# A trunk kernel whose first RMS norm is scaled in transposed form, with dummy products while x loads and a new order of the first transfers

## The chip, the cores and the metric

The kernel runs on one core of one Trainium2 chip. A core has a matrix engine (TensorE, PE in the rows; PEld is its weight load), VectorE (DVE), ScalarE (ACT), GpSimd (POOL) and SyncE (SP), a large on-chip buffer of 128 partitions (SBUF), and eight PSUM banks of 128 x 512 float32 in which products are summed. Engines run their own lists of instructions in order and wait for one another on semaphores. The metric is the device time of one execution in microseconds (us). The kernel before takes 1001.04 us, the median of three runs (1000.92 to 1001.54).

## The reference

A trunk of two layers on 256 tokens of width 1024, all in float32. Each layer is half a SwiGLU feed-forward (FFN), a mixing block (retention, block-sparse attention and a convolution, side by side), and half an FFN again; each of the three starts with an RMS norm of x, and one more norm ends the trunk. The model width is 1024 and an FFN's inner width 2816. This case is about the first norm and the first columns of the first FFN (left out below: the mixing block, whose result is added to x):

```python
def rms_norm(x, g):
    xf = x.astype(jnp.float32)
    y = xf * lax.rsqrt(jnp.mean(xf * xf, -1, keepdims=True) + EPS)
    return (y * g.astype(jnp.float32)).astype(x.dtype)

def swiglu(h, wg, wu, wd):
    return (jax.nn.silu(h @ wg) * (h @ wu)) @ wd

for l in range(DEPTH):
    h = rms_norm(x, ffn1_norm[l])
    x = x + 0.5 * swiglu(h, ffn1_wg[l], ffn1_wu[l], ffn1_wd[l])
    h = rms_norm(x, mix_norm[l])
    ...
    h = rms_norm(x, ffn2_norm[l])
    x = x + 0.5 * swiglu(h, ffn2_wg[l], ffn2_wu[l], ffn2_wd[l])
return rms_norm(x, final_norm)
```

## The kernel before

**Numbers in two parts.** Products keep float32 accuracy by splitting each operand into a high part (a rounded copy, type fp32r) and a low part (what the rounding left). ScalarE writes the high part (`whi` of a weight at L145, `hT` or `hfh` of an activation at L196), VectorE subtracts it from the source to get the low part (`wlo` at L146, `hT` or `hfl` at L197). A product is then three products, high by high, high by low and low by high (`mm3`, L201 to L203), or two of which the first takes both parts of the activation at once (`mm2w`, L207 and L208).

**The stream of weights.** All weights pass in a fixed order through three buffers of 1 MB (`raw`). `fetch` issues a transfer on SyncE's queue; the first two are cut into four parts of 256 KB each. `pump` splits half a buffer (a piece of 1024 columns) into its two parts; at most ten pieces are in store (`WBUFS`). The products call `tick`, which pumps the next piece and moves on the side chains of work that wait for their turn.

**The first norm.** `x` stands in two tiles, `x[0]` and `x[1]`, of 128 tokens each. The norm's vector `g` is loaded in a form in which all 128 partitions hold all 1024 numbers (512 KB). For each half of the columns of `x[t]`, ScalarE squares with a running sum (L338, into `sq`), VectorE multiplies x by g (L339, into `xr`), GpSimd adds the constant and takes the power -1/2 (L344, `r`), VectorE multiplies `xr` by `r` (L348), TensorE transposes four blocks of 128 x 128 into one PSUM bank named `tr` (L354), and `split` (L196, L197) takes the bank of 512 columns out as the high and low parts of `hT`, the transposed activation.

**The first FFN's start.** `first_pair` computes gate and up of the first 256 of 2816 columns: for `x[0]`, then for `x[1]`, eight blocks k of 128 columns of x by three products of 512 columns each (L201 to L203). The chain `gated` then forms `s` and `h` (L401, L402) and transposes `h` (L405). After that `single(j)` runs for j = 2 to 21 with products for both token tiles together (L207, L208), each one bank for the gate (`mm`) and one for up (`tr`); with ScalarE and VectorE joining the two halves of a bank (L212, L213).

**What sets the order.** From L831 on to the end of `first_pair` the program's order is the order in which the code is written, engine by engine (`ordered(True)`), as it is at some later stretches; in the others (`ordered(False)`) a scheduler sets it. In `run`, four pieces are pumped around the norm of `x[0]`, and the transposes of `x[1]` are a side chain (`rest`, started at L852) that counts calls of `tick`: `x[1]`'s first four transposes stand in front of block k6 of `x[0]`, the next four behind k7. Small constants (`pos`, `inv`, `vec`, `decay`, `mask`) are issued in `setup_late`, which is called in the loop's second round, behind `single(5)`, and the next norm's vector is loaded through ScalarE's queue (`nxt.gain()`, L363) into the same buffer `g`.

## Time and profile before

| | |
|---|---|
| median of three runs | 1001.04 us (1000.92 to 1001.54) |
| the profiled execution | 1000.19 us, with a span of 998.4 us |
| mean granted clock of TensorE | 0.998 |
| busy: PE, DVE, ACT, POOL | 981.6 us (98%), 685.5 (69%), 537.9 (54%), 64.1 (6%) |
| moved by DMA | 180.69 MB, a mean of 181 GB/s |

The span is the time from the first to the last instruction of the profiled execution; the execution's own time is 1.8 us more. "Busy" counts the time in which an engine works on an instruction. The busy shares are means over the whole span; the rows below mostly come from its first 80 us. A row of a timeline gives the start, the time, the engine, the line of the code, the operation with output and inputs, and behind "x" how many instructions of the kind stand together; in brackets the idle time before, with what ended it.

### The profile page before, as it was taken

The numbers are of one execution on the slowest core, as the hardware profiler recorded it, in microseconds if no ns is written. First come the engines' busy times: TensorE is split into PE (matmuls) and PEld (weight loads), VectorE is DVE, ScalarE is ACT, GpSimd is POOL, SyncE is SP. The second block draws the span as 40 slices with busy tenths as digits, with TensorE's granted clock in tenths as the row PEclk, the third lists the DMA queues.
The fourth block names the chain that finished last, engine by engine and source line by source line (L and its number), as shares of the span: only waits on it lengthen the run. The fifth ranks groups of instructions, "written<-read, shape, count | busy, mean of one in ns | idle before, by whom it ended". The sixth has DMA issues, their size and how long they took to land.

```text
span 998.4 us, 13763 instructions
## 1 busy us (share of the span) xinstructions
PE 981.6 (98%) x5312; PEld 847.6 (85%) x5312; DVE 685.5 (69%) x1032; ACT 537.9 (54%) x904; POOL 64.1 (6%) x109
## 2 busy tenths in 40 slices
PE   6999999999999999999999999999999999999997
PEld 5888888898998888888888888888989888888885
DVE  6886565569976866666576656566699677666653
ACT  6755555366554755555465545454665456555542
POOL 1000000021141000000000000002100400000000
PEclk9999999999999999999999999999999999999999
DMA  8955554336441855555546555544545347555511
GB/s 309 347 194 201 175 204 156 142 122 214 170 170 64 302 204 172 201 177 199 181 173 218 179 193 186 188 150 139 186 143 197 138 148 253 175 204 174 205 44 43
DMA packets 28722, 180.69 MB, mean 181 GB/s; under 512 B 3440, under 2 KB 3824, under 8 KB 10480
## 3 DMA queue, kind: packets, MB, share of 16 engines
q1 hardware_dynamic: 27360, 176.07, 50.7%
q10 hardware_dynamic: 1296, 3.74, 1.0%
q8 instruction: 42, 0.69, 0.3%
q14 instruction: 24, 0.20, 0.1%
HBM read 178.74 MB, written 1.05 MB: 180 GB/s over the span
## 4 chain that ended last, share of the span: by engine, by line
PE 90%; DVE 6%; DMA 1%; ACT 1%; issue 1%; SPq 0%; POOL 0%; POOLq 0%; ACTq 0%; DVEq 0%
PE tr L207 15%; PE mm L207 15%; PE acc L451 8%; PE acc L448 8%; PE acc L447 8%; PE tr L208 7%; PE mm L208 7%; PE mm L201 4%; PE mm L202 4%; PE mm L203 4%; DVE wlo L146 3%; DVE ac L695 2%; PE acc L207 1%; PE tr L354 1%; PE acc L638 1%
## 5 line engine op out<-in xcount | busy, mean ns | idle before, releaser
L146 DVE TENSOR_TENSOR wlo<-raw,whi 128x1024 fp32r<-128x1024 f32 (+2 forms) x348 | 403.3, 1171 | 184.1 <-ACT whi L145 180.3
L145 ACT ACTIVATE whi<-raw 128x1024 fp32r<-128x1024 f32 (+2 forms) x348 | 348.6, 1013 | 229.0 <-PE acc L451 92.3
L207 PE MATMUL tr<-hT,whi 128*128 128x512 f32 x640 | 228.0, 397 | 0.2 <-DVE hfl L197 0.2
L207 PE MATMUL mm<-hT,whi 128*128 128x512 f32 x640 | 227.3, 396 | 0.0
L208 PE MATMUL mm<-hT,wlo 128*128 128x256 f32 x640 | 178.7, 279 | 0.0
L208 PE MATMUL tr<-hT,wlo 128*128 128x256 f32 x640 | 178.7, 279 | 0.0
L207 PEld LDWEIGHTS tr<-hT,whi 128*128 128x128 f32 x640 | 120.2, 188 | 29.2 <-PE mm L208 0.4
L207 PEld LDWEIGHTS mm<-hT,whi 128*128 128x128 f32 x640 | 120.2, 188 | 28.5
L447 PE MATMUL acc<-whi,hfh 128*128 128x512 f32 x352 | 139.2, 395 | 0.0
L448 PE MATMUL acc<-wlo,hfh 128*128 128x512 f32 x352 | 138.7, 394 | 0.0
L208 PEld LDWEIGHTS mm<-hT,wlo 128*128 128x128 f32 x640 | 120.6, 189 | 1.5
L208 PEld LDWEIGHTS tr<-hT,wlo 128*128 128x128 f32 x640 | 120.7, 189 | 0.0
L451 PE MATMUL acc<-whi,hfl 128*128 128x512 f32 x352 | 115.8, 396 | 0.0
L201 PE MATMUL mm<-whi,hT 128*128 128x384 f32 (+1 forms) x288 | 106.7, 371 | 0.7 <-ACT hT L196 0.7
L203 PE MATMUL mm<-whi,hT 128*128 128x384 f32 (+1 forms) x288 | 101.2, 351 | 0.0
L202 PE MATMUL mm<-wlo,hT 128*128 128x384 f32 (+1 forms) x288 | 101.1, 351 | 0.0
L447 PEld LDWEIGHTS acc<-whi,hfh 128*128 128x128 f32 x352 | 66.5, 189 | 15.1
L451 PEld LDWEIGHTS acc<-whi,hfl 128*128 128x128 f32 x352 | 66.3, 188 | 15.2
L448 PEld LDWEIGHTS acc<-wlo,hfh 128*128 128x128 f32 x352 | 66.3, 188 | 13.7
L433 ACT ACTIVATE s<-part 128x256 f32<-128x256 f32 x80 | 33.2, 414 | 79.2 <-DVE part L213 79.1
L213 DVE TENSOR_TENSOR part<-part,tr 128x256 f32<-128x256 f32 x80 | 33.6, 420 | 47.1 <-ACT part L212 47.1
L201 PEld LDWEIGHTS mm<-whi,hT 128*128 128x128 f32 x288 | 54.7, 190 | 5.5 <-issue 1.3
(151 smaller groups left out, 954.2 us busy)
## 6 DMA issues: line engine op xcount, KB each, us to landing
raw<-in_wgb SPq DMA_DIRECT2D x80, 1024.0 KB, 4.9
raw<-in_wd SPq DMA_DIRECT2D x44, 1024.0 KB, 4.9
raw<-in_win SPq DMA_DIRECT2D x28, 768.0 KB, 4.6
raw<-in_wout SPq DMA_DIRECT2D x8, 1024.0 KB, 4.8
raw<-in_wga SPq DMA_DIRECT2D x6, 1024.0 KB, 5.3
raw<-in_wcv SPq DMA_DIRECT2D x4, 1024.0 KB, 4.8
raw<-in_wga SPq DMA_DIRECT2D x8, 256.0 KB, 6.9
g<-in_fgain ACTq DMA_DIRECT2D x3, 512.0 KB, 3.5
```

What stands on the lines that cost most here:

```text
L145: nc.scalar.activation(hi[:, c], src, AF.Copy)
L146: nc.vector.tensor_tensor(lo[:, c], src, hi[:, c].bitcast(F32), op=OP.subtract)
L201: mm(out, ah, wh, start=start, stop=False)
L202: mm(out, ah, wl, start=False, stop=False)
L203: mm(out, al, wh, start=False, stop=stop)
L207: mm(out, wh, x, start=start, stop=False)
L208: mm(out[:, :S], wl, x[:, 0], start=False, stop=stop)
L213: self.nc.vector.tensor_tensor(v, lo, ps[:, :S], op=OP.add)
L433: nc.scalar.activation(s, v, AF.Silu)
L447: mm(ys[t][h], hi[:, ts], wh[:, n], start=first, stop=False)
L448: mm(ys[t][h], hi[:, ts], wl[:, n], start=False, stop=False)
L451: mm(ys[t][h], lo[:, ts], wh[:, n], start=False, stop=last)
```

## The change

The first norm gets code of its own, `start`, in the place of the lines L832 to L852.

- `gcol` is the first norm's vector as a tile of 128 partitions by 8 columns (4 KB), loaded through ScalarE's queue behind `ident`. The vector is no longer loaded in its 512 KB form.
- `spin(16)` is sixteen products of 512 columns on a tile `z` of ones (bf16, in the buffer of `sq`) into a bank `tr`, which nobody reads.
- `first_stats` squares as before but leaves out the multiplication by g; the second addition for `r` stands on VectorE. VectorE scales the first half of the columns by `r`; the second half is scaled on ScalarE for `x[0]` and on VectorE for `x[1]`.
- `first_T` takes each of the four blocks of a bank out by itself: a ScalarE copy with the column of `gcol` as its scale, then on VectorE (block times column) minus the high part.
- The order is new: the second weight piece is pumped between the two banks of `x[0]`, the norm of `x[1]` begins behind both banks, and the transposes of `x[1]` stand in front of block k4 (first four) and of block k6 of `x[0]`.
- `x[1]` is loaded in two transfers. `setup_late` waits, through a one-column copy on GpSimd into each constant's tile, for an `hf` tile of the first pair, and issues each constant behind it.
- The buffer `g` has no user before the next norm, so that norm's vector (`mgain`) is issued where nothing precedes it on ScalarE's queue.

```diff
@@ fetch
             if (i, j) == (0, 1):
-                self.nc.sync.dma_start(self.x[1], self.a["x"][1])
+                for h in range(2):
+                    c = slice(h * 512, (h + 1) * 512)
+                    self.nc.sync.dma_start(self.x[1][:, c], self.a["x"][1][:, c])
@@ setup, setup_late
         self.ident = self.load("ident", (P, P), eng=nc.scalar)
-
-    def setup_late(self):
-        self.pos = self.load("pos", (P, NT), I32)
-        self.inv = self.load("inv", (P, 40))
-        self.vec = self.load("vec", (P, NVEC))
-        self.decay = self.load("decay", (P, H * 2 * P))
+        self.gcol = self.load("gcol", (P, KT), eng=nc.scalar)
+
+    def spin(self, n):
+        ps = self.trb()
+        z = self.act.tile([P, 512], BF16, tag="sq", bufs=1, name=self.name("z"))
+        self.nc.vector.memset(z, 1.0)
+        for _ in range(n):
+            self.nc.tensor.matmul(ps, z[:, :P], z, start=True, stop=True)
+
+    def first_stats(self, t, n):
+        nc = self.nc
+        n["xr"] = n["tile"]()
...
+        for h in range(2):
+            sq = self.act.tile([P, 512], BF16, tag="sq", bufs=1, name=self.name("sq"))
+            nc.scalar.activation(sq, self.x[t][:, h * 512:(h + 1) * 512], AF.Square, scale=1.0 / 32.0, accum_out=ss[:, h:h + 1])
+        nc.gpsimd.tensor_scalar(e, ss[:, 0:1], EPS, None, op0=OP.add)
+        nc.vector.tensor_tensor(e, ss[:, 1:2], e, op=OP.add)
+        nc.gpsimd.tensor_tensor(r, e, self.mhalf[:, :1], op=OP.pow)
+        c = slice(0, 512)
+        nc.vector.tensor_scalar(n["xr"][:, c], self.x[t][:, c], r, None, op0=OP.mult)
+
+    def first_T(self, t, h, n, hT):
+        ps = self.trb()
+        for j in range(4):
+            k = 4 * h + j
+            self.nc.tensor.transpose(ps[:, j * P:(j + 1) * P], n["xr"][:, k * P:(k + 1) * P], self.ident)
+        for j in range(4):
+            k = 4 * h + j
+            g = self.gcol[:, k:k + 1]
+            src = ps[:, j * P:(j + 1) * P]
+            hi, lo = [x[:, k, t * P:(t + 1) * P] for x in hT[:2]]
+            self.nc.scalar.activation(hi, src, AF.Copy, scale=g)
+            self.nc.vector.scalar_tensor_tensor(lo, src, g, hi.bitcast(F32), op0=OP.mult, op1=OP.subtract)
+
+    def start(self, st):
+        self.spin(16)
+        self.fetch()
+        n0, n1 = st.state(0), st.state(1)
+        c = slice(512, 1024)
+        self.first_stats(0, n0)
+        self.pump()
+        self.nc.scalar.activation(n0["xr"][:, c], self.x[0][:, c], AF.Copy, scale=n0["r"])
+        self.first_T(0, 0, n0, st.hT)
+        self.pump()
+        self.first_T(0, 1, n0, st.hT)
+        self.first_stats(1, n1)
+        self.nc.vector.tensor_scalar(n1["xr"][:, c], self.x[1][:, c], n1["r"], None, op0=OP.mult)
+        self.pump()
+        self.pump()
+        self.done.add(st.mark(0))
+        self.hold = True
+
+        def rest():
+            yield 2
+            self.first_T(1, 0, n1, st.hT)
+            yield 1
+            self.hold = False
+            self.first_T(1, 1, n1, st.hT)
+            self.done.add(st.mark(1))
+
+        self.spawn(rest())
+
+    def setup_late(self, after):
+        def late(tile, src):
+            v = tile[:, 0:1]
+            self.nc.gpsimd.tensor_copy(v if tile.dtype == F32 else v.bitcast(F32), after[:, 0:1].bitcast(F32))
+            self.nc.sync.dma_start(tile, src)
+
         c = self.const
+        for n, shape, dt in (("pos", (P, NT), I32), ("inv", (P, 40), F32), ("vec", (P, NVEC), F32), ("decay", (P, H * 2 * P), F32)):
+            t = c.tile(list(shape), dt, tag=n, name=n)
+            late(t, self.a[n])
+            setattr(self, n, t)
...
-            self.nc.sync.dma_start(mask, self.a["mask"])
+            late(mask, self.a["mask"])
@@ ffn
                 if f == 0 and p == 2:
-                    self.setup_late()
+                    self.setup_late(hf[1][1])
@@ run
         self.setup()
-        st = steps[0]
-        st.g = self.gain(st.src, self.nc.sync, 2)
-        self.fetch()
-        n0, n1 = st.state(0), st.state(1)
-        self.norm_half(0, 0, st.g, n0)
-        self.norm_half(0, 1, st.g, n0)
-        self.norm_scale(0, n0)
-        self.norm_scale(1, n0)
-        self.pump()
-        self.norm_T(0, 0, n0, st.hT)
-        self.norm_T(0, 1, n0, st.hT)
-        self.norm_half(1, 0, st.g, n1)
-        self.norm_half(1, 1, st.g, n1)
-        self.pump()
...
-        self.spawn(st.rest(1, n1))
+        self.start(steps[0])
@@ host side
+    o["gcol"] = o["fgain"][0].reshape(KT, P).T
```

**ScalarE's order, from the program's start.** `x_78` is `x[0]` and `x_79` is `x[1]`; numbers behind a name count tiles. A wait names what must have come: Pool_49, PE_49, DVE_49 and Activation_49 count finished instructions of an engine, a DMAHW a transfer. Before:

```order
L226 ACT_TABLE_LOAD
L226 ACTIVATE warm<-mhalf 128x8 [waits Pool_49]
L218 DMA ident<-in_ident 128x128
L338 ACTIVATE sq_98,ss_95<-x_78 128x512 [waits DMAHW0_49]
L338 ACTIVATE sq_102,ss_95<-x_78 128x512 [waits DMAHW1_49,Activation_49]
L145 ACTIVATE whi_116<-raw_87 128x512 [waits DMAHW5_49]
L145 ACTIVATE whi_116<-raw_87 128x512 [waits DMAHW6_49]
L196 ACTIVATE hT_93<-tr_122 128x4x128 [waits PE_49]
L196 ACTIVATE hT_93<-tr_129 128x4x128 [waits PE_49]
L338 ACTIVATE sq_140,ss_137<-x_79 128x512 [waits DMAHW7_49,Activation_49]
```

After:

```order
L437 DMA g_319<-in_mgain 128x1024
L228 ACT_TABLE_LOAD
L228 ACTIVATE warm<-mhalf 128x8 [waits Pool_49]
L220 DMA ident<-in_ident 128x128
L220 DMA gcol<-in_gcol 128x8
L253 ACTIVATE sq_117,ss_114<-x_78 128x512 [waits DMAHW1_49,DVE_49,PE_49]
L253 ACTIVATE sq_119,ss_114<-x_78 128x512 [waits DMAHW2_49,Activation_49]
L147 ACTIVATE whi_132<-raw_105 128x512 [waits DMAHW3_49]
L147 ACTIVATE whi_132<-raw_105 128x512 [waits DMAHW4_49]
L280 ACTIVATE xr_113<-x_78,r_116 128x512 [waits Pool_49]
L270 ACTIVATE hT_112<-tr_139,gcol 128x128 [waits DMAHW7_49,PE_49]
L270 ACTIVATE hT_112<-tr_139,gcol 128x128 [waits DVE_49] x3
```

The next norm's vector moved to the front, the first square gained a wait for TensorE and VectorE, a scaling of `xr` stands ahead of the first copy out of PSUM, and that copy became four, of which three wait for VectorE; the squares of `x[1]`, tenth before, come later than the rows printed.

**VectorE's order, from the first weight piece's low part on.** Before:

```order
L146 TENSOR_TENSOR wlo_117<-raw_87,whi_116 128x512 [waits DMAHW5_49,Activation_49]
L146 TENSOR_TENSOR wlo_117<-raw_87,whi_116 128x512 [waits DMAHW6_49,Activation_49]
L197 TENSOR_TENSOR hT_93<-tr_122,hT_93 128x4x128 [waits Activation_49]
L197 TENSOR_TENSOR hT_93<-tr_129,hT_93 128x4x128 [waits Activation_49]
L339 TENSOR_TENSOR xr_136<-x_79,g_84 128x512 [waits DMAHW7_49,DVE_49]
L339 TENSOR_TENSOR xr_136<-x_79,g_84 128x512
L146 TENSOR_TENSOR wlo_150<-raw_87,whi_149 128x512 [waits DMAHW0_49,Activation_49]
L146 TENSOR_TENSOR wlo_150<-raw_87,whi_149 128x512 [waits DMAHW1_49,Activation_49]
L348 TENSOR_SCALAR xr_136<-xr_136,r_139 128x512 [waits DVE_49,Pool_49]
L348 TENSOR_SCALAR xr_136<-xr_136,r_139 128x512 [waits DVE_49]
```

After:

```order
L148 TENSOR_TENSOR wlo_133<-raw_105,whi_132 128x512 [waits DMAHW3_49,Activation_49]
L148 TENSOR_TENSOR wlo_133<-raw_105,whi_132 128x512 [waits DMAHW4_49,Activation_49]
L271 SCALAR_TENSOR_TENSOR hT_112<-tr_139,gcol,hT_112 128x128 [waits DMAHW7_49,Activation_49]
L271 SCALAR_TENSOR_TENSOR hT_112<-tr_139,gcol,hT_112 128x128 [waits Activation_49] x3
L148 TENSOR_TENSOR wlo_153<-raw_105,whi_152 128x512 [waits DMAHW1_49,Activation_49]
L148 TENSOR_TENSOR wlo_153<-raw_105,whi_152 128x512 [waits DMAHW2_49,Activation_49]
L271 SCALAR_TENSOR_TENSOR hT_112<-tr_158,gcol,hT_112 128x128 [waits Activation_49] x4
L255 TENSOR_TENSOR e_173<-ss_172,e_173 128x1 [waits Activation_49,Pool_49]
L258 TENSOR_SCALAR xr_171<-x_79,r_174 128x512 [waits DMAHW6_49,Pool_49]
L285 TENSOR_SCALAR xr_171<-x_79,r_174 128x512 [waits DMAHW0_49]
```

Each subtraction of 512 columns became four that wait for ScalarE, the second weight piece moved between the two banks, and the scaling of `x[1]` stands behind both.

**TensorE's order, around the first transposes of `x[1]`.** Before:

```order
L201 MATMUL mm_179<-whi_159,hT_93 128x512 [waits Activation_49]
L202 MATMUL mm_179<-wlo_160,hT_93 128x512 [waits DVE_49]
L203 MATMUL mm_179<-whi_159,hT_93 128x512
L354 MATMUL tr_198<-ident,xr_136 128x128 [waits PE_49]
L354 MATMUL tr_198<-ident,xr_136 128x128 x3
L201 MATMUL mm_179<-whi_165,hT_93 128x512 [waits Activation_49]
```

After:

```order
L203 MATMUL mm_206<-whi_152,hT_112 128x512 [waits Activation_49]
L204 MATMUL mm_206<-wlo_153,hT_112 128x512 [waits DVE_49]
L205 MATMUL mm_206<-whi_152,hT_112 128x512
L264 MATMUL tr_219<-ident,xr_171 128x128 [waits DVE_49]
L264 MATMUL tr_219<-ident,xr_171 128x128 x3
L203 MATMUL mm_206<-whi_186,hT_112 128x512 [waits Activation_49]
```

Before, the transposes stand behind blocks k4 and k5 (the third weight piece, `whi_159`); after, behind k2 and k3 (the second, `whi_152`), and they wait for VectorE.

## Rows read from the trace of the kernel before

**Rows 1.** Page, part 4: shares of the chain that ended last, by engine.

```profile
PE 90%; DVE 6%; DMA 1%; ACT 1%; issue 1%; SPq 0%; POOL 0%; POOLq 0%; ACTq 0%; DVEq 0%
```

**Rows 2.** Waits of TensorE, whole run: total us, times, longest us.

```profile
PE tr L354 <- DVE xr L348: 8.5, 3, 8.1
...
PE mm L201 <- ACT hT L196: 0.7, 1, 0.7
```

**Rows 3.** Timeline of TensorE: start us, us, then the instruction.

```profile
10.70 0.80 PE L201 MATMUL mm<-whi,hT 128*128 128x512 f32 x1 [0.66 <-ACT hT L196]
...
25.36 0.39 PE L207 MATMUL mm<-hT,whi 128*128 128x512 f32 x1
```

**Rows 4.** Chain in order of time, 0 to 26 us: start us, us.

```profile
3.05 6.46 DMA raw<-in_wga
...
15.16 0.43 PE mm L201
...
15.89 0.23 PE mm L203
...
17.50 0.44 PE tr L354 x4
```

**Rows 5.** Busy us by stretch: window, PE, PEld, DVE, ACT, POOL, PEclk, DMA.

```profile
10.00:25.36 15.36, 14.70 (x60) 11.35 (x59) 13.99 (x21) 12.66 (x22) 1.82 (x3) 1.00 0.95 340
```

**Rows 6.** Timeline of VectorE, 7 to 22 us.

```profile
7.53 0.88 DVE L348 TENSOR_SCALAR xr<-xr,r 128x512 f32<-128x512 f32 x2
...
10.19 0.69 DVE L146 TENSOR_TENSOR wlo<-raw,whi 128x512 fp32r<-128x512 f32 x1 [1.18 <-ACT whi L145]
...
15.20 2.49 DVE L146 TENSOR_TENSOR wlo<-raw,whi 128x512 fp32r<-128x512 f32 x4
...
19.56 1.23 DVE L146 TENSOR_TENSOR wlo<-raw,whi 128x1024 fp32r<-128x1024 f32 x1 [0.26 <-ACT whi L145]
...
21.30 0.41 DVE L402 TENSOR_TENSOR h<-s,mm 128x256 f32<-128x256 f32 x1
```

**Rows 7.** Groups by shape, 0 to 80 us: busy us, mean ns, idle before.

```profile
L197 DVE TENSOR_TENSOR hT<-tr,hT 128x512 fp32r<-128x512 f32 x4 | 2.7, 686 | 0.9 <-ACT hT L196 0.9
...
L196 ACT ACTIVATE hT<-tr 128x512 fp32r<-128x512 f32 x4 | 2.3, 591 | 2.6 <-PE tr L354 2.6
...
L344 POOL TENSOR_TENSOR r<-e,mhalf 128x1 f32<-128x1 f32 x2 | 1.5, 737 | 0.2
...
L197 DVE TENSOR_TENSOR hfl<-tr,hfh 128x256 fp32r<-128x256 f32 x2 | 0.8, 416 | 0.0
...
L196 ACT ACTIVATE hfh<-tr 128x256 fp32r<-128x256 f32 x2 | 0.7, 370 | 0.0
```

**Rows 8.** Timeline of ScalarE, 9 to 15 us.

```profile
9.53 0.63 ACT L145 ACTIVATE whi<-raw 128x512 fp32r<-128x512 f32 x1 [1.27 <-DMA raw<-in_wga]
10.07 1.06 ACT L196 ACTIVATE hT<-tr 128x512 fp32r<-128x512 f32 x2
11.02 0.63 ACT L338 ACTIVATE sq<-x 128x512 bf16<-128x512 f32 x1
...
12.31 0.19 ACT L338 ACTIVATION_READ_ACCUMULATOR sq<-x 128x1 f32 x1
12.40 2.70 ACT L145 ACTIVATE whi<-raw 128x512 fp32r<-128x512 f32 x5
```

**Rows 9.** DMA issues, 0 to 60 us: KB each, median us to landing.

```profile
ident<-in_ident ACTq DMA_DIRECT2D x1, 64.0 KB, 3.7
```

**Rows 10.** Timelines of VectorE and TensorE at one PSUM bank.

```profile
32.46 0.41 DVE L213 TENSOR_TENSOR part<-part,tr 128x256 f32<-128x256 f32 x1
...
33.98 0.39 PE L207 MATMUL tr<-hT,whi 128*128 128x512 f32 x1
```

**Rows 11.** Timeline of SyncE (the DMA queue), 50 to 56 us.

```profile
50.65 0.42 SPq L243 DMA_DIRECT2D mask<-in_mask  x1
55.97 0.33 SPq L125 DMA_DIRECT2D raw<-in_wgb  x1
```

More of the change, by code (lines that the diff above doesn't have):

```diff
@@ new lines, in first_stats @@
+    def first_stats(self, t, n):
+        nc = self.nc
+        n["xr"] = n["tile"]()
+        ss = self.small.tile([P, 2], F32, tag="ss", name=self.name("ss"))
+        e = self.small.tile([P, 1], F32, tag="e", name=self.name("e"))
+        r = n["r"] = self.small.tile([P, 1], F32, tag="r", name=self.name("r"))
+        for h in range(2):
[6 more added lines that the diff above has]
+        nc.vector.tensor_scalar(n["xr"][:, c], self.x[t][:, c], r, None, op0=OP.mult)
@@ L831, in run @@
         self.setup()
-        st = steps[0]
-        st.g = self.gain(st.src, self.nc.sync, 2)
-        self.fetch()
-        n0, n1 = st.state(0), st.state(1)
-        self.norm_half(0, 0, st.g, n0)
-        self.norm_half(0, 1, st.g, n0)
-        self.norm_scale(0, n0)
-        self.norm_scale(1, n0)
-        self.pump()
-        self.norm_T(0, 0, n0, st.hT)
-        self.norm_T(0, 1, n0, st.hT)
-        self.norm_half(1, 0, st.g, n1)
-        self.norm_half(1, 1, st.g, n1)
-        self.pump()
-        self.norm_scale(0, n1)
-        self.norm_scale(1, n1)
-        self.pump()
-        self.pump()
-        self.done.add(st.mark(0))
-        self.hold = True
-        self.spawn(st.rest(1, n1))
+        self.start(steps[0])
         for l in range(L):
```

## The prediction

> **What bounds the kernel now.** I read the engines' shares first, then who waited for whom, and then only the stretch in which TensorE waits. TensorE holds 90% of the chain that ended last [rows 1]. Of all its waits over the whole run, 8.1 us is the wait for the first transposes' input, and no other single wait is over 0.7 us [rows 2]. So nearly all that this change can move is when TensorE gets through its first stage: from the start to the first product of the stage that follows, `single(2)`, at 25.36 us [rows 3]. A product that starts there later makes the end later by as much, since nothing behind it waits long enough to give time back.
>
> In that stage there are three marks. The first weight product starts at 10.70 [rows 3], behind a weight transfer that landed at 9.51 [rows 4]. Products run at 0.43 us each until about 15.6 and at 0.23 us after that [rows 4], which are the two levels of 512 columns at 1.2 and 2.4 GHz. And from 10 to 25.36 VectorE is busy for 13.99 and ScalarE for 12.66 of 15.36 us [rows 5]: the products share this stage with the splitting of weights and activations into a high part (ScalarE) and a low part (VectorE), and those two have little room. I call a block of 128 columns of x a block, k0 to k7, and the 128 tokens of `x[0]` and `x[1]` the first and the second half.
>
> **The change part by part.**
>
> *Start.* The dummy products need the memset of `z` on VectorE, from about 0.8 on, when the engines are up; a subtraction over 512 columns takes 0.69 [rows 7], no memset of that size is in the trace, and I take 0.25 between 0 and 0.69. Sixteen products at 0.43 from 1.1 on end at 8.0; with the change of pace 4.9 us after steady work began, as at 10.70 to 15.6, they end at 7.1, and all at 0.23 would end at 4.8. I take 7.1, from the same kind of work. `z` lies in the buffer of `sq`, so the first square on ScalarE now waits for the last dummy product (the PE wait in the order). Before, it waited for x alone; now it starts at 7.15. Two squares take 1.48 (11.02 to 12.50) [rows 8] and end at 8.65. The last addition moves from GpSimd to VectorE (I take 0.2), the power stays on GpSimd at 0.74 [rows 7], so `r` is there at 9.7. VectorE scales 512 columns in 0.44 [rows 6], and four transposes take 0.44 warm [rows 4]: the first PSUM bank is ready at 10.65. The other way to the same point gives the same: ScalarE's second weight copy waits for a transfer that landed at 9.51 and ends at 10.16 [rows 4, 8], and its new pass over the second half of xr (0.55) stands in front of the first hT copy, at 10.7. So the first hT copy comes at **10.7, against 10.07** before [rows 8], whether or not the dummy products end earlier than I think; if they end at 8.0, it is 11.4.
>
> The first transfers carry the same bytes: 0.5 MB of vector leaves SyncE's queue, but the next norm's vector (0.5 MB), which before was issued late in the stage, now stands first in ScalarE's queue. Before, 64 KB on that queue took 3.7 us beside x [rows 9], so the two queues share the DMA engines. x then lands perhaps 1.5 us later, which the wait for the dummy products covers; the second weight piece has the same 1.6 MB in front as before, so I leave it at 9.5. The new column vector (4 KB) is issued at about 1.6; at the 3.7 of the small transfer it is there at 5.3, at twice that at 9.0, before its use at 10.7; beyond that each us late is a us of the end.
>
> *Scaling as the transposes leave PSUM.* Before, a bank of four blocks left in one ScalarE copy (0.591) and one VectorE subtraction (0.686) [rows 7]. Now each block is one of each, and in the order every ScalarE copy but the first of a bank waits for VectorE, and every subtraction for its copy: the two take turns. A 128x128 step is not in the trace. ScalarE: 0.370 for 256 and 0.591 for 512 columns give 0.26 for 128 on a straight line, VectorE 0.416 and 0.686 give 0.28, and a hand-over took 0.03 (10.16 to 10.19) [rows 6, 7, 8]. One step is 0.26 + 0.28 + 0.06 = **0.60**. Bounds: in proportion to columns 0.15 + 0.17 + 0.06 = 0.38; at the price of 256 columns 0.85. Four steps are 2.4 us for a bank, in which each engine stands idle for more than half, against 1.3 before.
>
> That the two take turns the waits in the order show; no row of before has four such steps. The Trainium skill ("PSUM — Partial Sum Buffer", PSUM bank collisions raise a hardware error) says why: any two engines' accesses to one bank, reads as well, are kept apart by a dependency. Without that rule a bank would take about 1.3 us here, as in the first rival below.
>
> *The ladder that follows, engine by engine.* First bank: VectorE finishes the second low weight piece at 11.35, so the bank ends on ScalarE at 13.1 and on VectorE at 13.4. ScalarE copies weights for k2 and k3 (0.54 each, 2.70 for 5 [rows 8]) to 14.15, VectorE subtracts them (0.62 each, 2.49 for 4 [rows 6]) to 14.95. Second bank: to 16.7 and 17.0. Only then does ScalarE square the second half, 16.6 to 18.1; before it did that at 11.02. With 1.0 for sum and power and 0.44 for scaling, the second half's transposes start at **19.6, against 17.5** before [rows 4], and they stand earlier in TensorE's order: before k4, not before k6. TensorE has done k0 to k3 by 15.6 and waits 4 us there. Behind the wait stand four of the eight blocks of the first half. VectorE goes on: second scaling to 19.9, low parts of k4 to k7 (2.49) to 22.35, and then eight steps for the second half, some 7 x 0.60 after the first: to 26.4. Then come, in order, the next weight piece (ScalarE 26.0 to 27.1, VectorE 1.23 [rows 6]) to 28.4 and the gated product `h` (0.41) to 28.7. TensorE needs `h` for two transposes that stand in front of the last two blocks: 28.75 + 0.22 + 6 x 0.23 = **30.35 against 25.36: 5.0 later**.
>
> *What is late next.* VectorE reaches `h` at 28.3, 7.0 later than before (21.30 [rows 6]), while TensorE is 5.0 later. Before, VectorE left a bank at 32.87 that TensorE wrote again at 33.98, 1.1 us of room [rows 10]. Now 7.0 - 5.0 - 1.1 leaves a stall of 0.9 there; 0 if VectorE catches up in its idle time before it, up to 2 if ScalarE is late too. I take **0.7**.
>
> *What costs nothing.* The clock: with the dummy products the pace is up from the start, but the first half's products wait for VectorE in any case, and the second half's ran at 0.23 before. The late constants move some 30 us back on SyncE's queue: five issues of 0.42, 2.1 us, in a gap of 5 us between two weight transfers (50.65 to 55.97 [rows 11]); the five small copies on GpSimd stand in nobody's way. VectorE's first use of them, the mask, stands one weight piece and two sums further back in its order than before; if that did not cover it, VectorE would stop for up to the 3.7 of a small transfer [rows 9], with weight pieces in store for TensorE. Four multiplications by the vector (0.69 each) leave VectorE; their 2.75 is already left out of the ladder. Later stages keep TensorE's order.
>
> *Sum.* 5.0 + 0.7 = **5.7 us later**. The profiled execution took 1000.19 us (span 998.4), so 1005.9; the median of the runs before is 0.85 above it, which gives **1006.7**.
>
> **The rivals.**
> 1. *It does what it seems to be for (faster).* If the two engines did not take turns and the second half's squares came by 12 us, only TensorE would bound the stage: 10.7 + 48 x 0.23 + 2 x 0.44 + 0.22 = 22.8, 2.6 earlier, 998.4. It decides at 1.3 us for a bank instead of 2.4. Against it: the waits in the order, and VectorE's 13.99 of 15.36. Chance 0.08.
> 2. *No difference.* The steps cost their lower bound (0.38; some 14 of them stand on the path: -3.1) and the stall does not come (-0.7): +1.9 at most. Chance 0.06.
> 3. *Shorter steps, still slower.* Steps of 0.45 give 14 x -0.15 = -2.1: 1004.6. Chance 0.2, steps above 0.7 the same on the other side, 0.1.
> 4. *The pace falls back while TensorE waits 4 us for the second half.* No row of before has TensorE waiting that long after 15.6. Then it works from 19.6 at 0.43 and 0.22 for 4.9 us as at the start, four transposes and nine products, to 24.5; three products and four transposes warm to 25.6; 18 x 0.23 to 29.8, where the forecast stands at 28.75: +1.0, 1007.7. Chance 0.2.
>
> Beside rival 4: the Trainium skill ("TensorE: Matmul & The Clock Gate", What's actually happening) says that half rate is the resting state and activity lifts it. By that rule the dummy products' gain is lost again in that wait, as in rival 4, and the sum would be its 1007.7; nothing here shows it yet.
>
> **How the numbers follow.** Forecast as worked out 0.36; rivals 3 and 4 end on its side, in all 0.86 for slower by over 0.2% (about what a measurement of this kernel can tell from no change), 0.06 within it, 0.08 faster. The range goes from +2.4 (steps of 0.45, no stall, rounded down) to +7.5 (rival 4, dummy products all at 0.43 for +0.8): 1003.4 to 1008.5.
>
> **What would show it.** In the profile after: the first hT copy at about 10.7; steps of 128x128 copies and subtractions 0.60 apart; the second half's transposes waiting for VectorE's xr until about 19.6, with the wait of TensorE there about 4 us; the first product of `single(2)` at about 30.4. It is wrong if the subtractions overlap the copies of the same bank, if the second half's squares come by 13 us, or if that first product starts before 26.

## The result: 7.6 us slower, and where the time went

The changed kernel takes 1008.55 us (median of 6 runs, 1007.93 to 1009.45), the kernel before 1000.98 us in the same comparison (6 runs, 999.74 to 1002.28). The ratio is 1.0076, with a 95% interval from 1.0066 to 1.0087: slower, by 6.6 to 8.7 us. The forecast was 1006.7 us, with a range up to 1008.5. The direction and the mechanism came as forecast; the size, +7.6 against +5.7 us, was too small, and the time lies 0.05 us above the range. The term that was priced too low above all is the step in which ScalarE and VectorE take turns: 0.60 us forecast, 0.785 measured.

The profiled execution of the changed kernel took 1009.45 us, the longest of its six, with a span of 1007.7 us; that of before took 1000.19 us, with a span of 998.4, less than its median. So the two spans are 9.3 us apart where the medians are 7.6 apart, and a difference between two traces is read here as where time goes, not as how much.

The chain of the page (part 4) moved 2% of the span from TensorE to DMA and ScalarE, beside [rows 1]:

```profile
PE 88%; DVE 6%; DMA 2%; ACT 2%; issue 1%; POOL 0%; POOLq 0%; ACTq 0%; DVEq 0%
```

The waits of TensorE over the whole run (us in total, times, longest), beside [rows 2]. The wait of 8.1 us became one of 3.0 and a new one of 4.2 for the second half's transposes. The second row lies at 533 us, in the second layer (0.2 before); the stall behind the stage, at 38 to 43 us, that was priced at 0.7 is not among the waits:

```profile
PE tr L264 <- DVE xr L258: 7.2, 2, 4.2
...
PE tr L209 <- DVE hfl L199: 0.5, 1, 0.5
```

TensorE's timeline shows where the stage got longer. The first product of `single(2)` starts at 33.97, 8.6 us after the 25.36 of [rows 3]; the whole span is 9.3 longer, so 0.7 is lost in all that follows, 0.3 of it in that wait at 533 us:

```profile
1.44 6.51 PE L241 MATMUL tr<-z 128*128 128x512 bf16 x16 [1.44 <-DVE z L239]
10.96 1.97 PE L264 MATMUL tr<-ident,xr 128*128 128x128 f32 x8 [3.01 <-DVE xr L258]
12.58 0.78 PE L203 MATMUL mm<-whi,hT 128*128 128x512 f32 x1
...
21.77 1.12 PE L264 MATMUL tr<-ident,xr 128*128 128x128 f32 x4 [4.22 <-DVE xr L258]
...
33.97 0.40 PE L209 MATMUL mm<-hT,whi 128*128 128x512 f32 x1
```

ScalarE and VectorE in the first bank, beside [rows 6] and [rows 8]. A copy on ScalarE, a subtraction on VectorE, the next copy: 12.12, 12.52, 12.90, 13.30, so one block takes 0.785 us, and each engine stands idle for 0.42 to 0.43 between two of its own. What a row names as the end of that idle time is the other engine, every time. The last row shows where there is no turn: the fourth copy of one bank and the first of the next run back to back, though both write `hT`. So it is the bank that the two engines wait for, not the tile `hT`. ScalarE:

```profile
7.99 0.63 ACT L253 ACTIVATE sq<-x 128x512 bf16<-128x512 f32 x1 [5.32 <-PE tr L241]
...
12.12 0.37 ACT L270 ACTIVATE hT<-tr,gcol 128x128 fp32r<-128x128 f32 x1 [0.97 <-PE tr L264]
12.90 0.37 ACT L270 ACTIVATE hT<-tr,gcol 128x128 fp32r<-128x128 f32 x1 [0.42 <-DVE hT L271]
13.69 0.37 ACT L270 ACTIVATE hT<-tr,gcol 128x128 fp32r<-128x128 f32 x1 [0.42 <-DVE hT L271]
...
26.39 0.62 ACT L270 ACTIVATE hT<-tr,gcol 128x128 fp32r<-128x128 f32 x2 [0.42 <-DVE hT L271]
```

VectorE, with `h` at the end of the stage:

```profile
12.52 0.35 DVE L271 SCALAR_TENSOR_TENSOR hT<-tr,gcol,hT 128x128 fp32r<-128x128 f32 x1 [0.41 <-ACT hT L270]
13.30 0.35 DVE L271 SCALAR_TENSOR_TENSOR hT<-tr,gcol,hT 128x128 fp32r<-128x128 f32 x1 [0.43 <-ACT hT L270]
...
31.49 0.41 DVE L476 TENSOR_TENSOR h<-s,mm 128x256 f32<-128x256 f32 x1
```

The windows (busy time of PE, PEld, DVE, ACT, POOL, then the granted clock, DMA share, GB/s) show a granted clock of 0.50, the lower level, from 11.0 to 14.0, after TensorE had stood idle from 7.95 to 10.96, and again from 21.7 to 27.4, after the wait of 4.2 us. From 17.4 to 21.7 TensorE has nothing to do (0.16 us), ScalarE is busy for 3.49:

```profile
11.00:12.60 1.60, 1.60 (x9) 1.59 (x9) 1.19 (x3) 0.51 (x2) 0.00 (x0) 0.50 0.95 268
12.60:14.00 1.40, 1.40 (x5) 1.12 (x4) 0.62 (x2) 0.68 (x2) 0.00 (x0) 0.50 0.86 255
...
17.40:21.70 4.30, 0.16 (x1) 0.00 (x0) 1.66 (x6) 3.49 (x9) 0.80 (x2) 0.92 0.73 234
21.70:24.00 2.30, 2.23 (x8) 1.97 (x9) 2.30 (x6) 1.02 (x3) 0.00 (x0) 0.50 0.06 25
24.00:27.40 3.40, 3.40 (x12) 2.72 (x11) 2.09 (x6) 1.36 (x4) 0.00 (x0) 0.50 0.53 161
```

### The profile page after: what moved, and what is told of

Read it like the earlier page. It is cut to its first block, busy times and chain, and to the rows that moved or that the text cites. A ratio compares the mean times of both kernels' runs of the same rounds, so it can differ in the third digit from the quotient of the medians.

```text
span 1007.7 us, 13822 instructions
## 1 busy us (share of the span) xinstructions
PE 989.6 (98%) x5328; PEld 850.7 (84%) x5328; DVE 686.0 (68%) x1042; ACT 541.4 (54%) x917; POOL 66.0 (7%) x112
## 4 chain that ended last, share of the span: by engine, by line
PE 88%; DVE 6%; DMA 2%; ACT 2%; issue 1%; POOL 0%; POOLq 0%; ACTq 0%; DVEq 0%
PE tr L209 14%; PE mm L209 14%; PE acc L525 8%; PE acc L522 8%; PE acc L521 8%; PE tr L210 7%; PE mm L210 7%; PE mm L203 3%; PE mm L205 3%; PE mm L204 3%; DVE wlo L148 3%; DMA raw<-in_wgb 2%; DVE ac L769 2%; PE acc L209 1%; PE tr L428 1%
```

## The experiments

Each kernel was timed beside the kernel before on the same chip, whose medians were 1000.42 us (beside e1 to e4), 1000.58 (e5 to e8), 1000.83 (e9 to e12) and 1000.71 (e13 to e15), of 21 to 27 runs each. The changed kernel was timed in a comparison of its own, in which the kernel before took 1000.98 us. So a difference between e1, e2, e3, e6 or e15 and the changed kernel can be off by the 0.6 us by which the kernel before differs between comparisons. The edits to the changed kernel are diffs against it, the others against the kernel before.

### The turns of ScalarE and VectorE

In e2 nothing changes but the order in which eight instructions of a bank are written:

```diff
+        def block(j):
+            k = 4 * h + j
+            return self.gcol[:, k:k + 1], ps[:, j * P:(j + 1) * P], [x[:, k, t * P:(t + 1) * P] for x in hT[:2]]
+
         for j in range(4):
-            k = 4 * h + j
-            g = self.gcol[:, k:k + 1]
-            src = ps[:, j * P:(j + 1) * P]
-            hi, lo = [x[:, k, t * P:(t + 1) * P] for x in hT[:2]]
+            g, src, (hi, lo) = block(j)
             self.nc.scalar.activation(hi, src, AF.Copy, scale=g)
+        for j in range(4):
+            g, src, (hi, lo) = block(j)
             self.nc.vector.scalar_tensor_tensor(lo, src, g, hi.bitcast(F32), op0=OP.mult, op1=OP.subtract)
```

> The changed kernel with the four ScalarE copies of a bank written first and the four VectorE subtractions behind them, so that the two engines no longer take turns within a bank. Theory A (the turns of 0.79 us are most of the loss): a bank leaves ScalarE in about 1.1 to 1.5 us and VectorE in about 1.2 to 1.5, the second half's transposes start 2 to 3 us earlier than 21.77, single(2) starts at 30 to 31.5 instead of 33.97, and the time is 1005 to 1006.5. Rival B (the pace of TensorE, which falls back while it waits for the second half, is most of the loss): TensorE still waits, still restarts at 0.43 us, and the time is 1007.5 to 1008.5.

Measured: 1002.49 us (11 runs, 1001.51 to 1004.89), ratio to before 1.002 [1.0011, 1.0029]. That is 6.1 us below the changed kernel (5.6 by the two ratios), more than theory A asked for and far from B. On its trace the four copies of a bank go through in 1.14 us and the four subtractions in 1.12, where turns held both engines for 3.1. ScalarE's timeline:

```profile
10.18 1.14 ACT L271 ACTIVATE hT<-tr,gcol 128x128 fp32r<-128x128 f32 x4 [0.33 <-PE tr L264]
```

VectorE's, the same bank:

```profile
11.35 1.12 DVE L274 SCALAR_TENSOR_TENSOR hT<-tr,gcol,hT 128x128 fp32r<-128x128 f32 x4 [0.72 <-ACT hT L271]
```

TensorE's, the second half's transposes and `single(2)`:

```profile
17.19 0.66 PE L264 MATMUL tr<-ident,xr 128*128 128x128 f32 x4 [1.57 <-DVE xr L258]
...
26.98 0.40 PE L209 MATMUL mm<-hT,whi 128*128 128x512 f32 x1
```

The second half's transposes start at 17.19 instead of 21.77 and `single(2)` at 26.98 instead of 33.97. TensorE still loses its pace for a while in this run (the products at 11.75 to 14.5 took 0.43), so the pace is not what the 6 us were.

Two more kernels put the same two orders of instructions into the kernel before, to see whether the turns are dear by themselves or only where the change moved them. e11 takes the vector out of the norm of x and scales by `gcol` in turns, with weight pieces, squares and transposes where they stood before; e12 is e11 with the loop split as in e2:

```diff
-        st.g = self.gain(st.src, self.nc.sync, 2)
+        st.g = None
...
-        self.norm_T(0, 0, n0, st.hT)
-        self.norm_T(0, 1, n0, st.hT)
+        self.first_T(0, 0, n0, st.hT)
+        self.first_T(0, 1, n0, st.hT)
```

> The kernel before with the column of the vector as a scale on the way out of PSUM alone, block by block as in the changed kernel (no multiplication of x by the vector, no dummy products, weight pieces, squares and transposes in the order of before; the constants are issued late as in the change, since without the vector's transfer they would move in front of the weights). Theory A (the turns of 0.79 us cost by themselves, four banks of 3.1 us instead of 1.3, of which three lie on the path): 4.5 to 6.5 us slower than the kernel before. Rival B (it is the change's order of the pieces and transposes that makes the turns dear): 0 to 2 us slower.

> The same kernel with the four copies of a bank first and the four subtractions behind them. Theory A (a bank then costs ScalarE 1.1 and VectorE 1.1 us, 0.5 each more than in one piece, which the four saved multiplications of 0.69 give back on VectorE): within 1 us of the kernel before, up to 0.5 faster. Rival B (ScalarE, which does not get anything back and is busy for 12.66 of 15.36 us, becomes the bound): 1.5 to 2.5 us slower.

Measured: e11 1009.27 us (4 runs, 1008.82 to 1009.58), ratio 1.0084 [1.007, 1.0098]; e12 1001.54 us (11 runs, 1000.71 to 1002.44), ratio 1.0008 [0.9999, 1.0017]. So e11 is 8.4 us slower than the kernel before, more than the 4.5 to 6.5 expected, and 7.7 of them are the turns, by e12. The change's new order is not what made them dear. Without turns the column tile is worth nothing and costs next to nothing. The place on the trace of e11: two banks in turns last from 10.54 to 16.3 without a break, ScalarE comes to the squares of `x[1]` and the next weight piece only then, and TensorE waits for that piece, 4.0 us:

```profile
17.81 0.79 PE L201 MATMUL mm<-whi,hT 128*128 128x512 f32 x1 [3.95 <-ACT whi L145]
...
33.90 0.40 PE L207 MATMUL mm<-hT,whi 128*128 128x512 f32 x1
```

### Where the second half's transposes stand

e3 is the changed kernel with `x[1]`'s transposes in front of k6 and behind k7 again:

```diff
-            yield 2
+            yield 3
+            self.hold = False
             self.first_T(1, 0, n1, st.hT)
             yield 1
-            self.hold = False
             self.first_T(1, 1, n1, st.hT)
```

> The changed kernel with the transposes of x[1] where they stood before, in front of block k6 and behind k7 of x[0], so that TensorE can do k4 and k5 first. Theory A (VectorE's and ScalarE's work up to h sets the end of the stage, TensorE is only 0.4 us behind it): 0 to 0.6 us faster than the changed kernel, 1008.0 to 1008.5, and TensorE waits for h instead. Rival B (the wait of 4.2 us in front of the transposes is the loss itself): 2 to 4 us faster, 1004.5 to 1006.5.

Measured: 1009.63 us (4 runs, 1009.31 to 1010.38), ratio 1.0088 [1.0074, 1.0102], by the medians 1.1 us slower than the changed kernel: neither theory. B is refuted: the wait moves from the transposes to the weight piece behind them and costs as much. A was right that ScalarE and VectorE set the end, but took it that moving TensorE's transposes would leave their work as it is. On the trace TensorE waits 3.29 and 1.12 us for the third weight piece, ScalarE then stands idle for 3.81 us in front of the first copy of `x[1]`, whose transposes come later, and `h` is ready at 33.7 instead of 31.9, with TensorE waiting for it. ScalarE's timeline:

```profile
25.80 0.37 ACT L270 ACTIVATE hT<-tr,gcol 128x128 fp32r<-128x128 f32 x1 [3.81 <-PE tr L264]
```

TensorE's:

```profile
20.48 0.80 PE L203 MATMUL mm<-whi,hT 128*128 128x512 f32 x1 [3.29 <-ACT whi L147]
22.40 0.80 PE L204 MATMUL mm<-wlo,hT 128*128 128x512 f32 x1 [1.12 <-DVE wlo L148]
...
33.74 0.44 PE L479 MATMUL tr<-ident,h 128*128 128x128 f32 x2 [1.34 <-DVE h L476]
...
35.39 0.39 PE L209 MATMUL mm<-hT,whi 128*128 128x512 f32 x1
```

So the later place gains nothing while the engines take turns; that it costs about 1 us more is what the medians and this trace say (`single(2)` at 35.39 against 33.97), the two ratios' intervals overlap.

### The pace of TensorE in the wait

e6 is the changed kernel with seventeen dummy products, on a tile of their own, in front of the transposes of `x[1]`:

```diff
...
             yield 2
+            for _ in range(17):
+                self.nc.tensor.matmul(self.ys[1][1], z2[:, :P], z2, start=True, stop=True)
             self.first_T(1, 0, n1, st.hT)
```

> The changed kernel with seventeen more dummy products in front of the transposes of x[1], where TensorE waits from 17.5 to 21.8 us, so that its pace does not fall back there. Theory A (the work of ScalarE and VectorE up to h sets the end of the stage, h being ready at 31.9 where TensorE needs it at 32.37): 0.1 to 0.6 us faster than the changed kernel, 1008.0 to 1008.4. Rival B (the slow pace, fourteen products at 0.43 instead of 0.23, is lost in full): 2 to 3 us faster, 1005.5 to 1006.5.

Measured: 1008.24 us (5 runs, 1007.34 to 1009.17), ratio 1.0074 [1.006, 1.0088], 0.3 us below the changed kernel and within its spread: theory A. The pace did hold (granted clock 1.00 from 21.7 to 27.4, where the changed kernel has 0.50), and TensorE only came earlier to the wait for `h`, 1.86 us. The window first:

```profile
21.70:27.40 5.70, 5.59 (x28) 4.47 (x29) 4.28 (x10) 2.35 (x8) 0.00 (x0) 1.00 0.36 99
```

TensorE's timeline of the same run:

```profile
17.28 3.84 PE L296 MATMUL acc<-z 128*128 128x512 bf16 x17
21.66 0.66 PE L264 MATMUL tr<-ident,xr 128*128 128x128 f32 x4 [0.54 <-DVE xr L258]
...
31.86 0.44 PE L483 MATMUL tr<-ident,h 128*128 128x128 f32 x2 [1.86 <-DVE h L480]
```

### The dummy products at the start

e1 is the changed kernel without `self.spin(16)`; e7 is e1 with e2's order of the copies.

> The changed kernel (1008.55 us) without the sixteen dummy products, all else as it is. Theory A (the first square waits for the last dummy product, which ends at 7.95 us, and x has landed about 1.5 us before that): the first square starts at 6.4 to 6.6 us, the first copy out of PSUM at 10.6 to 11.0 instead of 12.12, and the kernel is 0.8 to 1.5 us faster than the changed one, 1007.0 to 1007.8. Rival B (the dummy products give more than they cost, because without them the first half's products run at 0.43 us for longer): 1008.5 to 1010.

> The changed kernel with the four copies of a bank first and without the dummy products: both edits that made it faster. Theory A (the two costs lie one behind the other and add up): 1.5 us below the kernel with the copies first, 1000.7 to 1001.3, no difference from the kernel before. Rival B (without turns TensorE is what ends last again, and its slow pace at the start, which the dummy products shorten, costs as much as their wait): 1002 to 1003.

Measured: e1 1007.06 us (5 runs, 1006.33 to 1007.52), ratio 1.006 [1.0047, 1.0074], 1.5 us below the changed kernel; e7 1001.62 us (11 runs, 1000.94 to 1004.22), ratio to before 1.0011 [1.0002, 1.002], 0.9 us below e2 and between its two theories. By the medians the dummy products cost 0.9 to 1.5 us; the intervals of each pair overlap, so the size is not certain. On the trace of e1 the first square starts at 6.59, as x lands, and the first copy out of PSUM at 11.02 (12.12 in the changed kernel). e15 asked whether it is the wait of the first square for their buffer that costs:

```diff
-        z = self.act.tile([P, 512], BF16, tag="sq", bufs=1, name=self.name("z"))
+        z = self.act.tile([P, 8192], BF16, tag="hT", bufs=2, name=self.name("z"))[:, :512]
```

> The changed kernel with the tile of the dummy products in a buffer of its own instead of that of the squares, so that ScalarE's first square waits for x alone. Theory A (the dummy products cost 1.5 us because the first square waits for their end): as fast as without them, 1006.8 to 1007.3, or up to 0.5 below, since the first half's products run faster. Rival B (they cost because TensorE is busy, or draw on something else): 1008.2 to 1008.8, as the changed kernel.

Measured: 1008.49 us (4 runs, 1007.69 to 1010.29), as the changed kernel: theory A fell, and by which path the dummy products cost what they cost is not settled. Yet on its trace the stage does what A said: first square at 5.81, first copy at 10.09, products at the fast pace from the first on up to the wait for the second half, `single(2)` at 31.80, 2.2 us before the changed kernel's 33.97. In that execution 1.5 us of it went again at a PSUM bank: a weight transfer landed at 37.80, ScalarE waited 2.60 us for it, VectorE read the bank late, and TensorE stood. ScalarE's timeline:

```profile
37.80 1.06 ACT L147 ACTIVATE whi<-raw 128x1024 fp32r<-128x1024 f32 x1 [2.60 <-DMA raw<-in_wgb]
```

TensorE's:

```profile
42.09 0.51 PE L209 MATMUL tr<-hT,whi 128*128 128x512 f32 x1 [1.46 <-DVE part L215]
```

In the changed kernel that transfer landed at 38.58, and ScalarE waited 1.20 us for it. Why it did not land earlier by as much as it was issued earlier stays open. What the row shows is that behind the stage a second limit is close: the weight buffers come free with VectorE's subtractions, and VectorE was held up. In the changed kernel no weight transfer stood in the queue for long parts of the time from 20 to 40 us (GB/s in 40 slices of 0.5 us):

```profile
GB/s 393 279 16 16 33 33 16 16 0 0 0 180 147 377 426 475 393 98 0 0 0 0 0 0 0 0 33 0 229 115 311 459 360 442 393 344 328 344 459 344
```

Alone, in the kernel before, the dummy products give nothing. e4 has sixteen of them on a buffer of their own, e5 five more behind the first transposes:

```diff
         self.setup()
+        self.spin(16)
         st = steps[0]
...
         self.norm_T(0, 1, n0, st.hT)
+        self.spin(5)
```

> The kernel before (1000.98 us) with the sixteen dummy products alone, on a tile in a buffer that nobody needs before the second norm. Theory A (the pace that TensorE reaches with the dummy products holds up to the first product at 10.7): products at 0.23 us from 10.7 on, TensorE then waits for VectorE's low parts until about 18, and 0.5 to 1.5 us are gained: 999.5 to 1000.5. Rival B (the pace falls back between the last dummy product at about 8 and the first products): 1000.8 to 1001.2, no difference.

> The kernel before with sixteen dummy products at the start and five more behind the first eight transposes, so that TensorE has work up to the first product (with the sixteen alone it stood idle from 9.46 to 11.26 us, and the products from 12.7 to 16 us ran at 0.43 us again). Theory A (that idle time is why the dummy products alone gave nothing): products at 0.23 us from the first one on, 0.5 to 1.2 us faster than the kernel before, about 999.5. Rival B (VectorE and ScalarE set the pace of this stage, TensorE waits for low parts instead): within 0.3 us of the kernel before.

Measured: e4 1001.18 us (11 runs, 1000.41 to 1002.08), ratio 1.0006 [0.9997, 1.0014]; e5 1000.98 us (11 runs, 999.83 to 1002.17), ratio 1.0002 [0.9993, 1.0011]. In e4 the pace was lost again: TensorE stood idle for 1.8 us in front of the first product, and the granted clock from 12.7 to 16.3 was 0.53. In e5 it held, and TensorE waited for VectorE's low parts instead, 0.38 and 1.17 us. e4's window:

```profile
12.70:16.30 3.60, 3.50 (x8) 1.95 (x7) 3.60 (x7) 3.48 (x8) 1.60 (x2) 0.53 0.92 340
```

e5's TensorE:

```profile
14.15 0.50 PE L202 MATMUL mm<-wlo,hT 128*128 128x512 f32 x1 [0.38 <-DVE wlo L146]
...
16.97 0.50 PE L202 MATMUL mm<-wlo,hT 128*128 128x512 f32 x1 [1.17 <-DVE wlo L146]
```

Theory B holds for both. In e5's trace the first product came at 11.37, 0.67 later than in [rows 3], behind a transfer of the vector, and the two waits for low parts are 1.55 us. So VectorE's work is what is late next as soon as TensorE is fast, but not VectorE alone: in front of the second of these low parts it had itself waited 0.74 us for GpSimd's power, since GpSimd's addition took 1.91 us in this execution and 0.69 in the kernel before. e5's VectorE, then GpSimd in e5 and in the kernel before:

```profile
15.43 0.88 DVE L356 TENSOR_SCALAR xr<-xr,r 128x512 f32<-128x512 f32 x2 [0.74 <-POOL r L352]
...
12.84 1.91 POOL L351 TENSOR_TENSOR e<-ss,e 128x1 f32<-128x1 f32 x1 [0.59 <-ACT sq L346]
...
12.64 0.69 POOL L343 TENSOR_TENSOR e<-ss,e 128x1 f32<-128x1 f32 x1 [0.59 <-ACT sq L338]
```

### Taking work off VectorE

If VectorE is the bound, work taken off it should bring out the dummy products' gain. e9 gives the two multiplications of `x[1]` by the vector to GpSimd; e10 does so with e5's dummy products:

```diff
...
-        nc.vector.tensor_tensor(n["xr"][:, c], x, g[:, c], op=OP.mult)
+        (nc.gpsimd if t == 1 and g is self.g0 else nc.vector).tensor_tensor(n["xr"][:, c], x, g[:, c], op=OP.mult)
```

> The kernel before with the two multiplications of x[1] by the norm's vector (2 x 0.64 us of VectorE at 12.0 to 13.3) moved to GpSimd, which is idle there. Theory A (TensorE, which is busy for 14.70 of 15.36 us in this stage at the slow pace of its start, sets the stage, and VectorE has just enough room): within 0.3 us of the kernel before. Rival B (VectorE sets it): 0.5 to 1.3 us faster.

> The same move to GpSimd, with the sixteen and five dummy products that keep TensorE's pace up to the first product. Theory A (with the pace kept, the two waits for VectorE's low parts, 1.2 and 0.4 us, were what took the gain): 0.8 to 1.3 us faster than the kernel before, 999.3 to 999.8. Rival B (the landing of the first transfers sets the stage): within 0.3 us of the kernel before.

Measured: e9 1001.66 us (11 runs, 1000.76 to 1002.87), ratio 1.0007 [0.9998, 1.0016]; e10 1001.48 us (11 runs, 1000.54 to 1002.68), ratio 1.0005 [0.9996, 1.0014]. No gain in either, as e9's theory A and e10's B say, but for other reasons than theirs: in e9's trace TensorE does wait for low parts (0.56 and 0.89 us). On the trace of e10 VectorE's two subtractions beside GpSimd's work took 2.02 us (1.29 in e5), the power behind the two multiplications ended at 15.5, and VectorE waited 0.47 us for it. GpSimd's timeline:

```profile
10.97 1.29 POOL L347 TENSOR_TENSOR xr<-x,g 128x512 f32<-128x512 f32 x1 [4.56 <-DVE wlo L146]
...
12.64 1.27 POOL L347 TENSOR_TENSOR xr<-x,g 128x512 f32<-128x512 f32 x1
13.87 0.64 POOL L351 TENSOR_TENSOR e<-ss,e 128x1 f32<-128x1 f32 x1
14.59 0.91 POOL L352 TENSOR_TENSOR r<-e,mhalf 128x1 f32<-128x1 f32 x1
```

VectorE's:

```profile
13.04 2.02 DVE L146 TENSOR_TENSOR wlo<-raw,whi 128x512 fp32r<-128x512 f32 x2 [0.97 <-ACT whi L145]
15.53 0.88 DVE L356 TENSOR_SCALAR xr<-xr,r 128x512 f32<-128x512 f32 x2 [0.47 <-POOL r L352]
```

Most of the 1.29 us taken off VectorE came back as longer subtractions and a wait, so e10 does not tell what would be the bound with less work on VectorE.

### The transfers

e8 has both transfer edits of the change in the kernel before, e13 the late constants alone, e14 `x[1]` in two transfers alone.

> The kernel before with the transfers of the change alone: x[1] in two transfers and the constants issued behind the copies on GpSimd. Theory A (they lie beside other work): within 0.3 us of the kernel before. Rival B (VectorE waits for a late constant, or the constants' 0.9 MB meets weights that are needed): 1 to 2 us slower.

> The kernel before with the constants issued late, and x[1] in one transfer as before. Theory A (the late constants lie beside other work; what the kernel with both lost came from x[1] in two transfers or from VectorE's order): within 0.5 us of the kernel before. Rival B (the constants are what cost): 1 to 1.8 us slower.

> The kernel before with x[1] in two transfers, and the constants as before. Theory A (one more issue of 0.45 us on SyncE's queue in front of the second weight buffer costs less than that): within 0.5 us of the kernel before. Rival B (the second half of x[1] and the weights behind it come late): 1 to 1.8 us slower.

Measured: e8 1002.02 us (11 runs, 1000.69 to 1007.06), ratio 1.0019 [1.0005, 1.0032]; e13 1001.76 us (11 runs, 1000.61 to 1003.17), ratio 1.0008 [0.9999, 1.0017]; e14 1000.83 us (11 runs, 999.55 to 1001.08), ratio 0.9996 [0.9987, 1.0005]. The halves of `x[1]` cost nothing. By its interval, e13 costs between nothing and 1.7 us; whether the late constants are what cost is not shown. In e13's trace the stall behind the stage is there, 1.93 us at 35.65, and a weight transfer precedes it, for which ScalarE waited 3.31 us. It landed at 29.86, and the late constants are issued only from 47 us on. In the kernel before, ScalarE did not wait for that transfer; in e8 it did, for 1.31 us. e13's ScalarE and TensorE:

```profile
29.86 1.06 ACT L145 ACTIVATE whi<-raw 128x1024 fp32r<-128x1024 f32 x1 [3.31 <-DMA raw<-in_wgb]
...
35.65 0.47 PE L207 MATMUL tr<-hT,whi 128*128 128x512 f32 x1 [1.93 <-DVE hfl L197]
```

How much of e8's and e13's numbers would belong to the change stays open.

No kernel here beats the kernel before: the nearest are e5 and e14, within their intervals of it.

## Why the prediction was right, and where it was wrong

**What held.** That the stage up to `single(2)` takes nearly all of the change (8.6 of 9.3 us between the traces), that ScalarE and VectorE take turns, that the second half's transposes then wait (4.2 us, forecast about 4), and that the ladder of ScalarE and VectorE sets when they start. Behind that the forecast took the ladder up to `h` as the path; in the trace of the changed kernel TensorE, at its slow pace, comes 0.5 us after `h`, and in e6, at its fast pace, it waits for `h` as forecast. The small stall behind it (0.7) did not come in the trace of the changed kernel; in e2's and e15's traces it is there, with 0.7 and 1.5. e2 and e11 against e12 show the turns as the cause: 6.1 and 7.7 us. The Trainium skill ("PSUM — Partial Sum Buffer", PSUM bank collisions raise a hardware error) says that the compiler's scheduler keeps accesses of two engines to one bank, reads too, apart by a dependency; the traces agree, both in the turns and in e2, where the first subtraction starts at 11.35 and the last copy of its bank has ended at 11.32.

**The step that failed: the price of a turn, 0.60 forecast, 0.785 measured.** It was made from a straight line through copies of 256 and 512 columns, 0.26 and 0.28 for 128. The length does not follow that line. 0.26 happens to be what one of several back-to-back instructions takes: four copies in 1.14 us in e2, a new one every 0.26. In turns the other engine waits for the end of the instruction, and a single copy of 128 columns is 366 ns long in both kernels, a subtraction 349 in the changed kernel and 343 in e2 (groups by shape, 0 to 36 us: busy us, mean ns, idle before). The changed kernel:

```profile
L270 ACT ACTIVATE hT<-tr,gcol 128x128 fp32r<-128x128 f32 x16 | 5.8, 366 | 8.1 <-DVE hT L271 6.5 <-PE tr L264 1.5
...
L271 DVE SCALAR_TENSOR_TENSOR hT<-tr,gcol,hT 128x128 fp32r<-128x128 f32 x16 | 5.5, 349 | 5.6 <-ACT hT L270 5.6
```

e2:

```profile
L271 ACT ACTIVATE hT<-tr,gcol 128x128 fp32r<-128x128 f32 x16 | 4.5, 366 | 1.5 <-PE tr L264 1.4
...
L274 DVE SCALAR_TENSOR_TENSOR hT<-tr,gcol,hT 128x128 fp32r<-128x128 f32 x16 | 4.5, 343 | 1.3 <-ACT hT L271 1.3
```

The copy of 256 columns in [rows 7] is 370 ns long, so the length hardly falls below 256 columns, and the upper bound of the prediction (0.85, the price of 256 columns) was the nearer row. 0.366 + 0.349 + 0.07 for two hand-overs is 0.785. The last leg, from the low parts of k4 to k7 to the last subtraction, was forecast at 4.05 us (22.35 to 26.4) and took 5.24 (24.52 to 29.76). The Trainium skill ("Perfetto Trace Analysis", Optimizing Scalar/DVE Operations) says that the profiled latency of such an instruction is about twice its fixed busy cost, because the half in which the write is acknowledged overlaps with the next instruction; the rows agree in kind: 0.366 and 0.343 long, 0.26 apart in e2; the factor is not shown here.

**The start, 10.7 forecast, 12.12 in the trace.** The dummy products ended at 7.95 (7.1 forecast), within the bound given, and the pace was then lost in the 3.0 us in which TensorE waited for `xr`, so that four transposes took 1.1 us instead of 0.44; the forecast had put the clock at no cost. The same sixteen products, all from 1.44 on, ended between 6.46 (e5) and 8.02 (e10) in the executions profiled here; the trace of the changed kernel is near the late end, which fits its being the longest of six; how late the dummy products ended in the median execution is not known.

**The pace (rival 4).** It came as described: granted clock 0.50 after the wait. Its price of 1.0 us did not: e6 is 0.3 us faster by the medians, and its `single(2)` starts 0.45 us earlier (33.52 against 33.97), since `h` was late too and TensorE had room to be slow. In the trace, TensorE passes the two transposes of `h` at 32.37, 0.5 us after `h` is there.

**The range.** It let one rival at a time happen. Longer steps, the later start and the slow pace came together: in the trace 30.35 became 33.97 by 1.4 (start), 0.8 (up to the second half's transposes, steps above all), 1.0 (from there to `h`, steps again) and 0.4 (pace). The text had named each by itself: 11.4 for the start with late dummy products (0.7), longer steps (at 0.79, 14 x 0.19 = 2.6), the slow pace (1.0). With all of them, 4.3, the upper end would have been 1011.

**Rival 1** took 1.3 us for a bank as the point from which the change is faster, and counted on no turns. Without turns a bank in e2 still lasts 2.3 us, from 10.18 to 12.47, since one engine follows the other, but each of the two is held for 1.1 us only. With that e2 and e12 come to 1002.5 and 1001.5 us and are not faster than before. The other half of that rival, the pace of TensorE from the start on, was tried in the kernel before, where it goes into waits for low parts (e5).

## What to carry to other kernels

When two engines read the same PSUM bank, write all of one engine's instructions on it before the first of the other's: alternating them in the code made each wait for the other, and the split of one loop into two was worth 6 to 8 us here. Price a step in which two engines take turns by the full length of one instruction on each, never by the spacing of a run of them or by a line through wider ones. Before warming an engine up, look at who is next: here the pace gained went into waits for VectorE's low parts, and in the changed kernel the dummy products cost time instead of giving any (0.9 to 1.5 us by the medians).

## What the runs showed of the hardware that was not expected

- Products of 512 columns took 0.43 us from 10.7 to 15.6 in the kernel before, the pace of the lower level (1.2 GHz), while the granted clock of that stretch is listed as 1.00; the same holds for the first dummy products. Later stretches of the same pace are listed at 0.50. So the listed clock did not show the slow pace at the start; the durations did. The window of the kernel before:

```profile
10.70:15.60 4.90, 4.90 (x11) 3.33 (x12) 4.90 (x10) 4.87 (x11) 1.82 (x3) 1.00 1.06 391
```

- TensorE's idle time of 3.0 us behind the dummy products cost the pace in the changed kernel and in e6, and 3.1 us did not cost it in e5 (granted clock 1.00 on, products at 0.23). In e2 the eight transposes behind 3.0 us still ran fast (1.09 us against 1.97), and the pace fell at the products behind them.
- Beside GpSimd's multiplications (1.27 to 1.29 us for 512 columns) VectorE's two subtractions of 512 columns took 2.02 us in e10 and 1.63 in e9, and 1.29 in the kernel before. Whether GpSimd's own work was slower for it is not shown: its power took 0.91 us in e10, but in the kernel before it took 0.57 for one half and 0.91 for the other too.
